# Mixture-of-experts stage: experts taken by token count, the last four on 64 token slots, weights split two pieces ahead

## The chip, the core and the metric

The kernel runs on one core of one Trainium2 chip. The metric is the device time of one execution in microseconds (us), the median of three runs. The core's engines work side by side, each with its own queue of instructions: TensorE (PE; its weight loads are listed as PEld), VectorE (DVE), ScalarE (ACT), GpSimd (POOL) and SyncE (SP), which here only issues transfers. Sixteen DMA engines carry what the queues issue.

## The reference

256 tokens of width 1024 go through a transformer block of two layers and then a second block of one layer. The part that the change touches most is the mixture of experts that ends the first block:

```
logits = (t @ w_router).astype(F32)                  # 8 experts
top_val, top_idx = lax.top_k(logits, TOP_K)          # 2 of them per token
top_w = jax.nn.softmax(top_val, axis=-1)
combine = jnp.sum(jax.nn.one_hot(top_idx, N_EXPERTS, dtype=F32) * top_w[..., None], axis=1)
for e in range(N_EXPERTS):
    gt, up = jnp.split(t @ w_gate_up[e], 2, axis=-1) # 1024 -> 2 x 3584
    y = (jax.nn.silu(gt) * up) @ w_down[e]           # 3584 -> 1024
    out = out + combine[:, e:e + 1].astype(t.dtype) * y
```

Each token needs two experts only, so an expert has some 64 tokens on the mean of the 256. The second block has an attention with a bias by relative position; its bias table of 8 x 384 numbers, copied to 128 rows of a scratch array in DRAM, is the other thing touched.

## The kernel before, in words

All weights are float32. TensorE multiplies in fp32r, and to keep the accuracy each factor is split into a high part H (a rounded copy, made on ACT) and a low part L (the rest, made on DVE; `parts`, lines 186 to 189). A product is three matmuls into one accumulator, H*H, H*L and L*H (`mm3`, lines 191 to 195): the 128 x 128 block of activations is the stationary factor, the 512 columns of weights move. `unit` (line 170) loads one piece of weights, 128 x 2048 numbers or 1 MB, into a buffer `raw`, and splits it in two halves of 1024 columns into `wH` (3 buffers) and `wL` (2 buffers). In the expert stage `raw` has 12 buffers in turns (`more_raw`, line 135): 5 of the ring, 5 of a pool of the stage, and 2 that are the second set of `hH` and `hL`.

In the expert stage the router's result is turned into `place`, the slot of each token among an expert's tokens. `pair` (line 988) gathers the tokens of two experts by matmuls with one-hot matrices `oh`, 128 slots each. For each of the 8 experts in the order of their numbers, and each of 7 slices j of 512 hidden columns, `up` (line 1070) makes gate and up product (4 pieces of `moe_w_gate_up`, 48 matmuls), then SiLU on ACT and the product on DVE (`act`), 4 transposes into `tp`, and the split into `aH` and `aL`; `down` (line 1105) of the slice before adds its 2 pieces of `moe_w_down` into two accumulators `acc` (24 matmuls). After an expert's last slice `scatter` (line 1130) splits the accumulators into `yH` and `yL`, multiplies with the transposed one-hot matrix and adds to the residual `xs` on DVE. The first gate product is made over all 256 tokens while the router's result is still on its way (`first_gates`, line 1049). An expert with more than 128 tokens would need a second pass, which stands behind a branch (`tc.If`, line 878) and would go over all eight experts again.

What stands behind what in an engine's queue is settled when the program is built; `issue_after(x)` keeps an instruction from being placed before x. In the dense layer ahead, `conditioning` (line 808) is work on the side: `side(j)` takes three steps of a generator per slice, and one of these steps is the copy of the bias table to 128 rows (line 859).

Of the kernel before, what the change touches and what calls it, by code (L numbers as in the profile page):

```python
# [10 lines left out]
F32 = mybir.dt.float32  # L11
# [19 lines left out]
RAW = 5  # L31
LEVELS = (64, 32, 16, 8, 4, 2, 1)
# [53 lines left out]
class Net:  # L86
# [47 lines left out]
    @contextmanager  # L134
    def more_raw(self, bufs, more):

        was, spare = self.ring, self.hp[1 - self.turn]
        with self.tc.tile_pool(name="more", bufs=more) as pool:
            more_ = lambda n: pool.tile([128, n], F32, name="raw", tag="raw")
            spare_ = [lambda n, tag=tag: spare.tile([128, n], F32, name="raw", tag=tag) for tag in ("hH", "hL")]  # L140
            turns = itertools.cycle([more_] * more + [was[0]] * bufs + spare_)
            self.ring = (lambda n: next(turns)(n)), *was[1:]
            yield
        self.ring = was
# [41 lines left out]
    def parts(self, H, L, src):  # L186

        self.high = self.nc.scalar.activation(H, src, AF.Copy)  # L188
        self.low = self.nc.vector.tensor_tensor(L, src, H.bitcast(F32), op=OP.subtract)  # L189
# [618 lines left out]
    def conditioning(self, sb, psum):  # L808
# [41 lines left out]
        def steps():  # L850
# [21 lines left out]
    def moe(self, f):  # L872
        nc, tc, A = self.nc, self.tc, self.A
        with self.stage("M", gu=2, acc=2) as (sb, psum):
            route = self.route(f, sb, psum)
            with self.more_raw(RAW, 5):
                self.experts(sb, psum, route, self.cst["iota"], f.x)
            with self.weights(1, 1, 1, 1024), tc.If(route["most"] > 128):

                iota2 = sb.tile([128, 128], F32, name="iota2", tag="before")  # L880
                nc.vector.tensor_scalar(iota2, self.cst["iota"], 128.0, None, op0=OP.add)
                self.experts(sb, psum, route, iota2)
# [13 lines left out]
    def route(self, f, sb, psum):  # L896
# [4 lines left out]
        before = sb.tile([128, NE, NE], F32, name="before", tag="before")  # L901
# [4 lines left out]
        nc.gpsimd.tensor_copy(ones, self.cst["ones"])  # L906
        hp = [sb.tile([128, 2, D], F32R, name=n) for n in ("hpH", "hpL")]
# [44 lines left out]
        route = dict(place=place, hp=hp, r=rp, r_token=r)  # L952

        def weights():
# [24 lines left out]
            most = sb.tile([128, 1], F32, name="most")  # L979
            nc.vector.tensor_reduce(most, ps[:, :NE], axis=AX.X, op=OP.max)  # L980
            most_i = sb.tile([128, 1], I32, name="most_i")
            nc.vector.tensor_copy(most_i, most)
            route["most"] = nc.values_load(most_i[0:1, 0:1], min_val=0, max_val=T)
# [4 lines left out]
    def pair(self, sb, psum, route, e, iota):  # L988
# [4 lines left out]
        oh = sb.tile([128, 2, 2, 128], F32R, name="oh")  # L993
        shape = [128, 2, 2, 128]
        nc.vector.tensor_tensor(oh, iota[:, None, None, :].to_broadcast(shape),
                                route["place"][:, :, e:e + 2, None].to_broadcast(shape), op=OP.is_equal)
        H, L = self.h_parts(other=False)
        g, hp = self.cols["moe_norm"], route["hp"]
        for c0 in range(0, KC, 2):
            ps = psum.tile([128, 512], F32, name="tp", tag="tp")  # L1000
            for k in (c0, c0 + 1):
                o = ps[:, (k - c0) * T:(k - c0 + 1) * T]
                for i in range(4):
                    nc.tensor.matmul(o, hp[i // 2][:, i % 2, k * 128:(k + 1) * 128],
                                     oh[:, i % 2].rearrange("p e s -> p (e s)"), start=i == 0, stop=i == 3)
                nc.scalar.activation(H[:, k], o, AF.Copy, scale=g[:, k:k + 1])  # L1006
                nc.vector.scalar_tensor_tensor(L[:, k], o, g[:, k:k + 1], H[:, k].bitcast(F32),
                                               op0=OP.mult, op1=OP.subtract)

        def later():  # L1010
            rs = sb.tile([128, 2], F32, name="r_slot", bufs=2)
            ps = psum.tile([128, 512], F32, name="r_ps", tag="tp")
            for i in range(4):
                nc.tensor.matmul(ps[:, i // 2 * 2:i // 2 * 2 + 2], oh[:, i % 2, i // 2], route["r"][:, i % 2],
                                 start=i % 2 == 0, stop=i % 2 == 1)
            nc.vector.tensor_reduce(rs, ps[:, :4].rearrange("p (e i) -> p e i", i=2), axis=AX.X, op=OP.add)
            return rs

        return (H, L), oh, later

    def experts(self, sb, psum, route, iota, x=None):
# [3 lines left out]
        W1, W2 = A["moe_w_gate_up"][0], A["moe_w_down"][0]  # L1025
        size = self.ring[2]
        ng = FE // 512
        acc, by = {}, {}

        def ohT(e):  # L1030

            if e % 2 == 0:
                by["ohT"] = sb.tile([128, 2, T], F32R, name="ohT")
                ps = psum.tile([128, 512], F32, name="tp", tag="tp")
                for i in range(4):
                    self.transpose(ps[:, i * 128:(i + 1) * 128], by["oh"][:, i % 2, i // 2].bitcast(F32))
                nc.scalar.copy(by["ohT"].rearrange("p e t -> p (e t)"), ps)
            return by["ohT"][:, e % 2]

        def halves(e, j, i):  # L1040

            n = size // 512
            c0 = i * FE + j * 512
            for k0 in range(0, KC, n):
                wH, wL = self.unit([(None, W1[e, k0 * 128:(k0 + n) * 128, c0:c0 + 512].rearrange(
                    "(c p) n -> p c n", p=128))], n, 512)
# [509 lines left out]
```

## Time and profile before

| | us |
|---|---|
| median of 3 runs (lowest to highest) | 1869.73 (1869.43 to 1871.19) |
| profiled execution | 1871.38 |
| its span, first to last instruction | 1869.2 |
| of it outside the span | 2.2 |
| expert stage, first gate matmul to the last addition to the residual | 514.5 to 1526.3 |

The page gives each engine's busy time, then the span in 40 slices. PE is busy for 97% of the span, DVE for 79%, ACT for 66%. Of the span, 1011.8 us lie in the expert stage. A matmul's duration in the trace overlaps that of the next one, so its price is the distance from one start to the next.

### The profile page before, as it was taken

To read this page: it belongs to the slowest core of one execution; us is meant where nothing else is said; L and a number is where in the kernel's file an instruction comes from. 1 tells how busy PE (TensorE), PEld (TensorE's weight loads), DVE (VectorE), ACT (ScalarE), POOL (GpSimd) and SP (SyncE) were. 2 spreads that over 40 slices of the span, in tenths; PEclk is the share of its full clock that TensorE was granted. 3 is DMA by queue.
4 is the path that set the end of the run, shared out by engine and by line. 5 is a ranking of instruction groups with operands and counts; after the bars stand their busy time and mean duration, and the time that the engine had idled before them with its cause. 6 is when DMAs were issued, how large, how long until landed. Compare 5 with 4: busy or idle time off the path is not lost. (4 is left out here: it accounts for less than half of the span.)

```text
span 1869.2 us, 23364 instructions
## 1 busy us (share of the span) xinstructions
PE 1809.2 (97%) x8491; PEld 1457.6 (78%) x8491; DVE 1477.4 (79%) x1819; ACT 1227.6 (66%) x1761; POOL 70.0 (4%) x107
## 2 busy tenths in 40 slices
PE   8999999999999999999999999999999979989997
PEld 6767787788778888788787887887887857778886
DVE  4857788676789999898988989888898876575555
ACT  5655444575678777777777777777787766555443
POOL 2002000110100000000000000000000010000001
PEclk9999999999999999999999999999999989999999
DMA  8537999642679999899999999998999945355551
GB/s 266 166 105 243 331 323 340 198 147 92 227 278 370 369 351 377 307 368 367 340 369 341 347 359 338 371 371 304 363 369 342 330 134 172 114 164 185 181 180 46
DMA packets 224938, 511.37 MB, mean 274 GB/s; under 512 B 10181, under 2 KB 35909, under 8 KB 221616
## 3 DMA queue, kind: packets, MB, share of 16 engines
q1 hardware_dynamic: 221872, 501.84, 75.8%
q0 software_dynamic: 2496, 7.10, 1.5%
q8 instruction: 69, 1.13, 0.2%
q10 hardware_dynamic: 448, 0.86, 0.1%
q14 instruction: 53, 0.43, 0.1%
HBM read 508.68 MB, written 2.66 MB: 274 GB/s over the span
## 5 line engine op out<-in xcount | busy, mean ns | idle before, releaser
L189 DVE TENSOR_TENSOR wL<-raw,wH 128x1024 fp32r<-128x1024 f32 (+1 forms) x1001 | 1072.2, 1117 | 199.8 <-issue 120.5
L188 ACT ACTIVATE wH<-raw 128x1024 fp32r<-128x1024 f32 (+1 forms) x1001 | 912.1, 969 | 252.5 <-PE gu L195 71.4
L193 PE MATMUL gu<-wH,hH 128*128 128x512 f32 x1192 | 468.0, 393 | 2.3 <-ACT hH L1006 2.3
L194 PE MATMUL gu<-wL,hH 128*128 128x512 f32 x1192 | 466.2, 391 | 3.1 <-DVE wL L189 3.0
L195 PE MATMUL gu<-wH,hL 128*128 128x512 f32 x1192 | 466.0, 391 | 0.0
L194 PEld LDWEIGHTS gu<-wL,hH 128*128 128x128 f32 x1192 | 224.5, 188 | 55.7 <-DVE wL L189 5.7
L195 PE MATMUL acc<-wH,aL 128*128 128x512 f32 x664 | 265.9, 401 | 0.0
L194 PE MATMUL acc<-wL,aH 128*128 128x512 f32 x664 | 264.0, 398 | 0.0
L193 PEld LDWEIGHTS gu<-wH,hH 128*128 128x128 f32 x1192 | 224.6, 188 | 50.3 <-ACT hH L1006 3.7
L195 PEld LDWEIGHTS gu<-wH,hL 128*128 128x128 f32 x1192 | 224.4, 188 | 46.1
L193 PE MATMUL acc<-wH,aH 128*128 128x512 f32 x664 | 257.3, 402 | 0.0
L193 PE MATMUL mm<-wH,hH 128*128 128x512 f32 (+1 forms) x384 | 152.5, 398 | 0.8 <-ACT hH L1484 0.5
L194 PE MATMUL mm<-wL,hH 128*128 128x512 f32 (+1 forms) x384 | 150.9, 393 | 0.0
L194 PEld LDWEIGHTS acc<-wL,aH 128*128 128x128 f32 x664 | 125.1, 188 | 32.3 <-DVE wL L189 4.1
L195 PE MATMUL mm<-wH,hL 128*128 128x512 f32 (+1 forms) x384 | 149.6, 391 | 0.0
L193 PEld LDWEIGHTS acc<-wH,aH 128*128 128x128 f32 x664 | 125.1, 188 | 26.2 <-issue 0.3
L195 PEld LDWEIGHTS acc<-wH,aL 128*128 128x128 f32 x664 | 125.1, 188 | 26.2 <-issue 0.2
L188 ACT ACTIVATE aH<-tp 128x512 fp32r<-128x512 f32 (+1 forms) x94 | 51.3, 545 | 121.4 <-PE tp L198 121.2
L193 PEld LDWEIGHTS mm<-wH,hH 128*128 128x128 f32 x384 | 73.7, 192 | 15.3 <-issue 1.7
L194 PEld LDWEIGHTS mm<-wL,hH 128*128 128x128 f32 x384 | 73.6, 192 | 14.6 <-issue 2.7
L195 PEld LDWEIGHTS mm<-wH,hL 128*128 128x128 f32 x384 | 73.4, 191 | 13.7 <-issue 1.7
L1093 DVE SCALAR_TENSOR_TENSOR act<-gu,r_slot,act 128x512 f32<-128x512 f32 x56 | 42.0, 750 | 49.1 <-PE gu L195 49.1
(437 smaller groups left out, 1415.8 us busy)
## 6 DMA issues: line engine op xcount, KB each, us to landing
raw<-in_moe_w_gate_up_dram SPq DMA_DIRECT2D x224, 1024.0 KB, 7.3
raw<-in_moe_w_down_dram SPq DMA_DIRECT2D x112, 1024.0 KB, 6.0
raw<-in_w_ff_dram SPq DMA_DIRECT2D x32, 1024.0 KB, 5.1
raw<-in_w_ada_dram SPq DMA_DIRECT2D x24, 1024.0 KB, 6.8
raw<-in_dense_w_gate_up_dram SPq DMA_DIRECT2D x44, 512.0 KB, 5.2
raw<-in_b_w_in_dram SPq DMA_DIRECT2D x12, 1024.0 KB, 5.1
raw<-in_w_in_dram SPq DMA_DIRECT2D x12, 1024.0 KB, 5.2
raw<-in_dense_w_down_dram SPq DMA_DIRECT2D x11, 1024.0 KB, 7.3
```

The lines of the kernel that those rows point to most:

```text
L188: self.high = self.nc.scalar.activation(H, src, AF.Copy)
L189: self.low = self.nc.vector.tensor_tensor(L, src, H.bitcast(F32), op=OP.subtract)
L193: mm(ps, xH, wH, start=start, stop=False)
L194: mm(ps, xH, wL, start=False, stop=False)
L195: mm(ps, xL, wH, start=False, stop=stop)
L1093: nc.vector.scalar_tensor_tensor(a, ps[1], r, a, op0=OP.mult, op1=OP.mult)
```

## The change

Six things are changed together.

- **Order of the experts.** Expert 0 stays first (its first gate product starts before the router's result is there); the other seven follow by falling number of tokens. DVE works the order out from the counts in 24 small operations behind the first slice (`order`), and SP loads the seven numbers and the largest count into registers; the address of every later piece of expert weights comes from such a register.
- **64 slots.** The last four experts in turn (`BIG_TURNS = 4`) have 64 slots. The stationary block then holds H in its first 64 columns and L in the other 64, so that one matmul with `wH` gives H*H in rows 0 to 63 and L*H in rows 64 to 127, and a second one with `wL` on 64 columns adds H*L: two matmuls for three. The two halves have to be added: for the gate by a copy to SBUF and a float32 matmul with a matrix `fold`, for the product behind the transposes (`both`), for the result by the scatter. The largest count is compared after 64 is added to those of the last four, so the second pass would run if one of the last four had more than 64 tokens.
- **Steps.** An expert's seven slices are taken in steps of 1, 2, 2 and 2; in a step of two a piece of `moe_w_gate_up` is 2 x 1024 columns, not 4 x 512.
- **Split ahead.** A piece is split whole (2048 columns), and two pieces ahead of the one that TensorE takes (`stream`, `ahead` = 2). `raw` has 10 buffers in turns, `wL` has 3. The evacuations of the accumulators (`act`, `aH`, `aL`, `yH`, `yL`, `xs`) stand behind these splits (`behind`, `put_off`).
- **Gathers.** Tokens are gathered for expert 0, for the next two, for the next one, and for the last four, not in four pairs.
- **Bias rows.** The copy of the bias table is made in 8 parts of 16 rows, one with each of the first 8 steps of the side work.

```
+BIG_TURNS = 4
...
+            spare_ = lambda n: spare.tile([128, n], F32, name="raw", tag="hL")
+            turns = itertools.cycle([more_] * more + [raw] * bufs + [spare_])
+            low_ = lambda n: whl[1].tile([128, n], F32R, name="wL")
+            spare_l = lambda n: spare.tile([128, n], F32R, name="wL", tag="hH")
+            lows = itertools.cycle([low_] * low + [spare_l])
...
+    def stream(self, sources, ahead):
+        nc = self.nc
+        raw_, (pH, lows), size = self.ring
+        low_ = lows if callable(lows) else lambda n: lows.tile([128, n], F32R, name="wL")
+        made = []
+        for src in sources:
+            raw = raw_(size)
+            view = lambda x: x.rearrange("p (c b) -> p c b", b=src.shape[-1])
+            nc.sync.dma_start(view(raw), src)
+            H = pH.tile([128, size], F32R, name="wH")
+            L = low_(size)
+            self.parts(H, L, raw)
+            made.append((view(H), view(L)))
+            if len(made) > ahead:
+                yield made.pop(0)
+        yield from made
...
-            nc.gpsimd.dma_start(self.skew, table[0].partition_broadcast(128))
-            yield
-            for seg in range(3):
-                yield from ada(seg)
-
+            copies = iter(range(0, 128, 16))
+            for _ in itertools.chain.from_iterable(ada(seg) for seg in range(3)):
+                i = next(copies, None)
+                if i is not None:
+                    nc.gpsimd.dma_start(self.skew[i:i + 16], table[0].partition_broadcast(16))
...
-            with self.more_raw(RAW, 5):
-                self.experts(sb, psum, route, self.cst["iota"], f.x)
+            with self.more_weights(RAW, 4, 2):
+                self.experts(sb, psum, route, self.cst["iota"], self.cst["iota"], 2, f.x)
             with self.weights(1, 1, 1, 1024), tc.If(route["most"] > 128):
...
+            nc.vector.tensor_scalar(cnt[:, 0:1], cnt[:, 0:1], 1000.0, None, op0=OP.add)
...
+            nc.vector.tensor_scalar(full[:, BIG_TURNS:], full[:, BIG_TURNS:], 64.0, None, op0=OP.add)
+            nc.vector.tensor_reduce(which[:, 0:1], full, axis=AX.X, op=OP.max)
+            whole = small("int", [NE], I32)
+            nc.vector.tensor_copy(whole, which)
+            sp = [mybir.EngineType.SP]
+            route["expert"] = [0] + [nc.values_load(whole[0:1, i:i + 1], engines=sp, min_val=0, max_val=NE - 1)
+                                     for i in range(1, NE)]
+            route["most"] = nc.values_load(whole[0:1, 0:1], min_val=0, max_val=T + 64)
...
+                if small:
+                    for x, d in ((H, slice(0, 2)), (L, slice(2, 4))):
+                        v = x[:, k].rearrange("p (e h s) -> p e h s", e=2, h=2)
+                        nc.scalar.activation(v[:, :, 0], o[:, d], AF.Copy, scale=g[:, k:k + 1])
+                        nc.vector.scalar_tensor_tensor(v[:, :, 1], o[:, d], g[:, k:k + 1], v[:, :, 0].bitcast(F32),
+                                                       op0=OP.mult, op1=OP.subtract)
...
+        steps = ((0,), (1, 2), (3, 4), (5, 6))
+        groups = ((0,), (1, 2), (3,), (4, 5, 6, 7))
...
+            pend = None
+            for e in range(NE):
+                for js in steps:
+                    yield from w1(e, js, 0)
+                    yield from w1(e, js, 1)
+                    if pend is not None:
+                        yield from w2(*pend)
+                    pend = e, js
+            yield from w2(*pend)
...
+        def behind():
+            with self.tc.issue_after(self.high.ins), self.tc.issue_after(self.low.ins):
+                yield
...
+        def product(ps, x, H, L, start, stop):
+
+            if len(x) == 2:
+                self.mm3(ps, *x, H, L, start, stop)
+                return
+            high = lambda: mm(ps, x[0], H, start=start, stop=stop)
+            if start:
+                high()
+            mm(ps[:64], x[0][:, :64], L, start=False, stop=False)
+            if not start:
+                high()
...
+            def fold():
+                for p in ps[0]:
+                    y = sb.tile([128, 512], F32, name="halves", tag="act", bufs=2)
+                    with behind():
+                        nc.scalar.copy(y, p)
+                    put_off(0, lambda p=p, y=y: mm(p, route["fold"], y, start=True, stop=True))
...
+                    if small:
+                        both = sb.tile([128, 4, 64], F32, name="both", tag="aL", bufs=2)
+                        nc.scalar.copy(both, pt[:, :, 64:])
+                        def add():
+                            with behind():
+                                nc.vector.tensor_tensor(both, pt[:, :, :64], both, op=OP.add)
+                            put_off(0, lambda: split(y[0][:, :, :64], y[0][:, :, 64:], both))
+                        put_off(0, add)
+                    else:
+                        self.split(*y, pt)
...
+                        if not started:
+                            activations()
+                            for g in range(len(js)):
+                                put_off(ahead - 1 + g, lambda g=g, parts=parts: parts(g))
+                            started = True
...
+                with behind():
+                    self.split(*y, acc[h])
+                put_off(ahead, lambda: scatter(h, y))
```

How the queues change, as the two programs are built. First VectorE, three slices in the middle of the expert numbered 5 before (`wL` is the low part of weights, `act` the product of the two halves, `aL` its low part):

```order
L189 TENSOR_TENSOR wL<-raw,wH 128x1024 x9
L1093 SCALAR_TENSOR_TENSOR act<-gu_9871,r_slot,act 128x512
L189 TENSOR_TENSOR wL<-raw,wH 128x1024 x2
L189 TENSOR_TENSOR aL<-tp,aH 128x512
L189 TENSOR_TENSOR wL<-raw,wH 128x1024 x10
```

And VectorE now, a step of two slices in the first of the last four turns (`both` adds the two halves, `aH<-both` is the low part):

```order
L215 TENSOR_TENSOR wL<-raw,wH 128x2048 x8
L1279 SCALAR_TENSOR_TENSOR act<-gu_8995,r_slot,act 128x512
L1279 SCALAR_TENSOR_TENSOR act<-gu_8996,r_slot,act 128x512
L215 TENSOR_TENSOR wL<-raw,wH 128x2048 x2
L1295 TENSOR_TENSOR both<-tp,both 128x256
L215 TENSOR_TENSOR wL<-raw,wH 128x2048
L1295 TENSOR_TENSOR both<-tp,both 128x256
L215 TENSOR_TENSOR aH<-both,aH 128x4x64
```

Between a product and what is made of it there stand now at least two whole pieces, and the work on a slice is three operations where there were two.

TensorE at the end of a gate product before, in expert 5:

```order
L193 MATMUL gu_10139<-wH,hH 128x512
L194 MATMUL gu_10139<-wL,hH 128x512
L195 MATMUL gu_10139<-wH,hL 128x512
L193 MATMUL acc_9828<-wH,aH 128x512
L193 MATMUL acc_9829<-wH,aH 128x512
L194 MATMUL acc_9828<-wL,aH 128x512
L195 MATMUL acc_9828<-wH,aL 128x512
```

And now, at the seam from gate (gu_8993, gu_8994) to up product (gu_8995, gu_8996) of the first of the last four turns:

```order
L1207 MATMUL gu_8995<-wH,hH 128x512
L1207 MATMUL gu_8996<-wH,hH 128x512
L1210 MATMUL gu_8995<-wL,hH 64x512 x2
L1207 MATMUL gu_8995<-wH,hH 128x512
L1210 MATMUL gu_8996<-wL,hH 64x512 x2
L1207 MATMUL gu_8996<-wH,hH 128x512
L1251 MATMUL gu_8993<-halves,fold 128x512
L1251 MATMUL gu_8994<-halves,fold 128x512
L1210 MATMUL gu_8995<-wL,hH 64x512
```

The third matmul of a product is gone, and the two matmuls that add the gate's halves stand a whole piece of the up product behind the gate.

## Rows read from the trace of the kernel before

**Rows 1.** The page, busy time of each engine over the whole span

```profile
PE 1809.2 (97%) x8491; PEld 1457.6 (78%) x8491; DVE 1477.4 (79%) x1819; ACT 1227.6 (66%) x1761; POOL 70.0 (4%) x107
```

**Rows 2.** Stretches: length, busy PE, PEld, DVE, ACT, POOL (count), PEclk, DMA share, GB/s

```profile
185.00:195.00 10.00, 10.00 (x47) 8.09 (x46) 9.90 (x10) 3.05 (x6) 0.55 (x1) 1.00 0.95 343
...
235.00:245.00 10.00, 10.00 (x45) 8.27 (x45) 9.25 (x8) 4.29 (x5) 1.01 (x2) 1.00 0.94 339
...
500.00:510.00 10.00, 10.00 (x50) 8.21 (x49) 7.57 (x10) 7.22 (x13) 0.00 (x0) 1.00 1.05 397
...
701.00:748.00 47.00, 47.00 (x212) 38.48 (x212) 42.85 (x40) 37.27 (x40) 0.00 (x0) 1.00 1.02 377
...
1042.00:1526.00 484.00, 478.41 (x2140) 386.36 (x2138) 429.06 (x415) 357.90 (x403) 0.00 (x0) 1.00 0.94 339
```

**Rows 3.** Who waited for whom, SP's DMA queue, 561 to 1496: total, times, longest

```profile
SPq L178 <- DVE wL L189: 773.7, 307, 8.2
```

**Rows 4.** Timeline of PE in the expert stage: start, us, engine, line, operation

```profile
514.50 0.40 PE L193 MATMUL gate<-wH,hH 128*128 128x512 f32 x1
...
1036.74 0.39 PE L195 MATMUL acc<-wH,aL 128*128 128x512 f32 x1
...
1044.16 0.39 PE L195 MATMUL gu<-wH,hL 128*128 128x512 f32 x1
...
1049.60 0.39 PE L195 MATMUL gu<-wH,hL 128*128 128x512 f32 x1
...
1051.23 0.60 PE L198 MATMUL tp<-cst,act 128*128 128x128 f32 x4
...
1052.14 0.39 PE L195 MATMUL acc<-wH,aL 128*128 128x512 f32 x1
...
1054.24 0.39 PE L195 MATMUL acc<-wH,aL 128*128 128x512 f32 x1
```

**Rows 5.** Timeline of DVE, expert 4 and the stage's end

```profile
1042.91 6.89 DVE L189 TENSOR_TENSOR wL<-raw,wH 128x1024 fp32r<-128x1024 f32 x6
...
1524.93 1.41 DVE L1142 SCALAR_TENSOR_TENSOR xs<-tp,comb,xs 128x512 f32<-128x512 f32 x2 [0.59 <-PE tp L1141]
```

**Rows 6.** Groups by line and shape, DVE and ACT: count, busy us, mean ns

```profile
L1093 DVE SCALAR_TENSOR_TENSOR act<-gu,r_slot,act 128x512 f32<-128x512 f32 x56 | 42.0, 750 | 49.1 <-PE gu L195 49.1
...
L189 DVE TENSOR_TENSOR aL<-tp,aH 128x512 fp32r<-128x512 f32 x72 | 49.3, 684 | 0.3 <-ACT aH L188 0.3
...
L1142 DVE SCALAR_TENSOR_TENSOR xs<-tp,comb,xs 128x512 f32<-128x512 f32 x32 | 22.6, 746 | 3.4 <-PE tp L1141 3.1
...
L189 DVE TENSOR_TENSOR aL<-tp,aH 128x256 fp32r<-128x256 f32 x22 | 9.1, 418 | 1.1 <-ACT aH L188 1.0
...
L189 DVE TENSOR_TENSOR ada_L<-ada_acc,ada_H 128x2048 fp32r<-128x2048 f32 x3 | 6.9, 2286 | 0.6 <-ACT ada_H L188 0.6
...
L188 ACT ACTIVATE ada_H<-ada_acc 128x2048 fp32r<-128x2048 f32 x3 | 5.7, 1915 | 7.6 <-DVE ada_acc L834 7.6
```

**Rows 7.** Groups by line and shape, PE: contraction*columns of the stationary, moving, mean ns

```profile
L193 PE MATMUL router<-hH,wrH 128*8 128x256 f32 x8 | 2.3, 290 | 0.0
...
L1004 PE MATMUL tp<-oh,hpL 128*128 128x256 f32 x64 | 13.1, 286 | 0.0
...
L310 PE MATMUL mem_s<-kvT,mem_qT 64*128 64x256 f32 x32 | 10.0, 428 | 0.0
```

**Rows 8.** The bias copy on POOL, PE's wait and the stretch around that wait

```profile
185.47 0.55 POOL L859 DMA_DIRECT2D skew<-skew_row  x1 [6.44 <-DMA skew_row<-skew_st]
...
208.61 0.69 PE L198 MATMUL tp<-cst,act 128*128 128x128 f32 x2 [4.20 <-DVE act L549]
...
205.00:215.00 10.00, 6.39 (x25) 5.19 (x25) 8.36 (x8) 4.83 (x6) 0.00 (x0) 0.83 0.97 343
```

**Rows 9.** Line 983: what SP spends on one register load and one address

```profile
L983 SPq TENSOR_LOAD <-most_i x1: 466/466/466, 546.5 to 546.5; - x1
...
L983 SPq FUSED_REGOPS  x1: 182/182/182, 547.0 to 547.0; - x1
```

More of the change, by code (lines that the diff above doesn't have):

```diff
@@ new lines, in experts, with take, put_off @@
+        stream = self.stream(sources(), ahead)
+        def take():
+            for i in range(len(later)):
+                later[i][0] -= 1
+            due = [x for x in later if x[0] < 0]
+            later[:] = [x for x in later if x[0] >= 0]
+            for x in due:
+                x[1]()
+            return next(stream)
+        def put_off(n, f):
+            later.append([n, f])
+        @contextmanager
+        def behind():
+            with self.tc.issue_after(self.high.ins), self.tc.issue_after(self.low.ins):
+                yield
@@ L1038, in ohT @@
[L1038 to L1046, printed above, removed]
-                yield from ((k0 + k, wH[:, k], wL[:, k]) for k in range(n))
+                for i in range(2 * n):
+                    self.transpose(ps[:, i * 128:(i + 1) * 128], oh[:, i % 2, i0 + i // 2].bitcast(F32))
@@ L1121, in experts @@
[L1121 to L1141 removed]
+                        product(acc[h], [y[:, k] for y in a], H[:, k - k0, d], L[:, k - k0, d],
+                                j == 0 and k == 0, j == steps[-1][-1] and k == 3)
@@ new lines, in down, with finish, half, scatter @@
+                yield
+        def finish(e):
+            acc, o = by.pop("acc"), ohT(e)
+            def half(h):
+                y = [sb.tile([128, 512], F32R, name=n) for n in ("yH", "yL")]
+                with behind():
+                    self.split(*y, acc[h])
+                put_off(ahead, lambda: scatter(h, y))
+            def scatter(h, y):
+                self.scatter(psum, h, y, o, route["comb"][:, :, e:e + 1], behind)
+                if h == 0:
+                    half(1)
+            half(0)
@@ new lines, in experts @@
+        made = {}
+        pend = None
+        for e, js in itertools.product(range(NE), steps):
+            activations, parts = up(e, js)
+            if js == steps[-1] and e + 1 in first:
+                ohT(e)
+                fetch(first[e + 1])
+            if pend is None:
+                activations()
+                for g in range(len(js)):
+                    parts(g)
+                if "comb" not in route:
+                    with self.tc.issue_after(self.low.ins):
+                        route["weights"]()
+            else:
+                started = False
+                for j in pend[1]:
+                    for _ in down(pend[0], j):
+                        if not started:
+                            activations()
+                            for g in range(len(js)):
+                                put_off(ahead - 1 + g, lambda g=g, parts=parts: parts(g))
+                            started = True
+                if pend[1] == steps[-1]:
+                    finish(pend[0])
+            pend = e, js
@@ new lines, in experts, with scatter @@
+        while later:
+            later.pop(0)[1]()
+        for j in pend[1]:
+            for _ in down(pend[0], j):
+                pass
+        finish(pend[0])
+        while later:
+            later.pop(0)[1]()
+    def scatter(self, psum, h, y, ohT, w, behind):
+        nc = self.nc
+        d = slice(h * 512, (h + 1) * 512)
+        for t in range(2):
+            ps = psum.tile([128, 512], F32, name="tp", tag="tp")
+            s = ohT[:, t * 128:(t + 1) * 128]
+            nc.tensor.matmul(ps, s, y[0], start=True, stop=False)
+            nc.tensor.matmul(ps, s, y[1], start=False, stop=True)
+            with behind():
```

277 lines of the change are left out of this document (168 added, 109 removed).

## The prediction

> **What bounds the kernel now.** I read the page's busy times first, then the stretches, then who waited for whom, then the timeline of TensorE and VectorE, and last the groups by line and shape, for durations. TensorE (PE) is busy for 97% of the span [rows 1]. The expert stage runs from PE's first gate matmul at 514.5 to the last addition to the residual, 1524.93 + 1.41 = 1526.3: 1011.8 us [rows 4, 5]. In its second half PE is busy for 478.4 of 484 us, but VectorE (DVE) is close behind with 429.1 [rows 2], so whatever PE gives up can be used only until DVE is full. The loads lead: SP spent 773.7 us of 935 waiting for DVE to free a buffer [rows 3].
>
> A slice can be counted from the timeline. From 1044.16 to 1049.60 stand 24 matmuls of the up product, 0.2267 each; from 1052.14 to 1054.24 nine of the down product, 0.2333 each; four transposes add some 0.45 [rows 4]. A slice of 48 + 24 matmuls is 10.88 + 5.60 + 0.45 = 16.93 us, an expert 118.5. Eight are 948 us of the 1011.8.
>
> **The change, part by part.** *TensorE, last four experts.* Two matmuls instead of three make 224 x 0.2267 + 112 x 0.2333 = 76.9 us per expert. That the one with 64 stationary columns costs as much as the one with 128 I take from the router's matmuls: 8 stationary columns 290 ns, 128 columns 286 ns, both moving 256 [rows 7]. The fold is a plain float32 matmul of 512 columns, which the trace does not show; the nearest row moves 256 in 428 ns where the split kind takes 286 [rows 7]. Its price lies between 0.23 (as any other) and 0.86 (twice the whole 428); I take 0.52, since 286 ns stands for a distance of 0.12 and 428 so for 0.26 per 256 columns. Seven folds are 3.6, seven slices of transposes 3.2, the scatter's 8 matmuls 2.1: 85.8 us per expert, 32.7 less than now. Its cover is DVE, below, so this alone is not the gain.
>
> *VectorE, last four experts.* Six back-to-back halves take 6.89 us and a lone one 1.22, so one starts every 1.134 and durations overlap by 0.08 [rows 5]. The whole piece exists in the trace as the split of `ada_acc`: 2.286 long [rows 6], 2.206 from start to start, against 2 x 1.134 = 2.268. An expert's 42 pieces are 92.7 us. Evacuations, each less 0.08 [rows 6]: `act` 0.67, and for `both` and the low part of `aH` 0.335 each by the row of 256 columns (418 ns): 1.34 per slice where there were 1.27. Scatter: four additions of 0.67 and two splits of 0.60, 3.9. That makes 92.7 + 9.4 + 3.9 = 106.0 us per expert: DVE loses almost nothing and becomes the bound, 106.0 against PE's 85.8. ScalarE has at most 42 x 1.915 = 80 us of splits [rows 6] and some 12 of copies; it stays behind DVE.
>
> *The last four in place.* In the built program DVE has split 175 of the 336 pieces when PE takes the fourth expert's last one. What is left: 161 x 2.206 = 355.2, 28 slices x 1.34 = 37.5, four scatters 15.5, together 408.2 us; then a tail of about 7 (the last piece's matmuls, and a scatter in two halves, one after the other, as now). In stretches in which DVE was the waited-for engine it was busy for 9.25 to 9.90 of 10 us [rows 2]; I take 0.96: 425 + 7 = 432. Before, the same way runs from 1036.74 + 0.39 = 1037.1 to 1526.3: 489.2 us [rows 4, 5]. Gain 57. With DVE never waiting it would be 415 (gain 74); the lower end is the loads' (below).
>
> *The loads, last four.* 161 pieces less the 9 that wait loaded are 152, or 159.4 MB. At the rate of one slice now, 6.29 MB in 16.93 us = 371 GB/s, they take 429 us; at the best long stretch, 377, 423; at the best short one, 397, 401 [rows 2]. The 371 was set by PE, not by the queue [rows 3], so I take the loads as just hidden by the 425, and 12 us for landing and tail where they are not: 441.
>
> The Trainium skill, "DMA: Bandwidth & Descriptors", "Specifications", gives 358 GB/s as the limit of HBM per core; by it the loads take 445 us, the last four 457, and the total would be 1827. The stretch of 377 over 47 us speaks against that limit here. The same page ("iDMA fabric") has a lone stream of 1 MiB loads with 4 KiB rows, the shape that most pieces now get, at 408.7; by that they take 390 and are hidden.
>
> *First four experts.* The same 504 matmuls each; PE stays the bound. Until the fourth's last product there are now 1037.1 - 514.5 = 522.6 us: 4 x 118.5, the first gates' 24 further matmuls and 4 selecting ones 6.3, three gathers of 32 x 0.12 = 3.8, three scatters of 2.1, 48 matmuls of the next expert 10.9: 509 of work, 13.7 of waits. Afterwards: 4 x 118.5, 6.3, two gathers of 3.8 and two of one expert each (32 x 0.11 by the transposes' distance) 3.5, three scatters 6.3, 32 matmuls of the next expert 7.3: 508.5. The waits can stay (0) or go (13.7), since scatter and gather now stand behind splits that are ready; I take half: gain 7.
>
> *Order and registers.* 24 small DVE operations fall into expert 0, where DVE has 118.5 - 106 = 12 us to spare: cost 0, some 4 us if that cover were gone. SP's eight register loads (0.47 + 0.18 and checks, some 0.7 each [rows 9], 5.5 together) hold up SP's queue; behind them stand 15 more pieces of expert 0. SP stops there before the 28th piece and DVE gives the result behind the 19th; a buffer for the 28th is free behind the 18th. A delay of one piece and 5.5 us meets up to nine loaded pieces, 25 us: hidden. Each later address costs SP 0.18, per piece of 2.5 us or more: hidden.
>
> *Bias rows.* The copy goes out at 185.47; at 208.61 PE has waited 4.20 us for DVE, which waited for weights, and in 205 to 215 it starts 25 matmuls, not the 46 or so of its neighbours, part of the time at the lower clock (mean 0.83) [rows 2, 8]. 21 x 0.2267 = 4.8. In eight parts the copy can cost nothing or the same, spread: gain 0 to 4.8, I take 4.
>
> **Sum.** 57 + 7 + 4 = 68 us. The span goes from 1869.2 to 1801, the profiled execution from 1871.4 to 1803; the median of the runs lies 1.7 below that execution: 1802.
>
> **Rivals.** *Loads take over.* Ten buffers for twelve, and a rate never seen for long. For it: the DMA engines are busy all the time at 377 already (share 1.02); against: 397 in a short stretch [rows 2]. 441 for the last four gives 1811; at the mean of the second half, 339, they would need 470 + 12 and give 1852.
>
> *Evacuations take over.* In the last four a slice has a longer chain (copy, fold, SiLU, product, transposes, copy, add, split), and DVE takes its queue in order: a product that is late holds back the splits behind it. For it: `act` waited 49.1 us for PE in 56 turns [rows 6]. Against: that was while PE was the bound, and two pieces now stand in between, over 4 us. 16 steps with two stops of 1.5 us are 48: 480, total 1850.
>
> *TensorE falls to its lower clock (slower than before).* PE will wait some (106 - 86) / 42 = 0.5 us at every piece. After the wait of 4.2 us the granted clock of 205 to 215 was 0.83 [rows 8], so some of that time was at 1.2 GHz. If the last four ran there throughout, PE would need 4 x 2 x 85.8 = 686 us: total 2055. It decides once PE needs more than 489 + 11 = 500 for the four, 1.46 times its 85.8. Against: waits of half a microsecond are an eighth of the one that did it, and at half speed PE would be busy all the time.
>
> *The second pass runs.* Counted from the reference on its own inputs, the experts have 55, 74, 53, 86, 71, 54, 55 and 64 tokens: turns 0, 3, 1, 4 and then 64, 55, 54, 53. The largest of the last four fills its slots exactly, 64 + 64 = 128 is not above 128. One token more and everything runs again, 352 MB or some 950 us at 371 GB/s: about 2750.
>
> **Chances.** My forecast 0.68, loads 0.15, evacuations 0.11, clock 0.04, second pass 0.02. My forecast's own range is 1777 (gains of 74, 14 and 5) to 1817 (the last four at 441, no wait gone in the first four). With the loads at their milder end and a part of the evacuations the range that holds 8 in 10 is 1783 to 1831. A measurement here tells 0.2% (3.7 us) from no change. Faster needs only that DVE, the loads or the chain leave 4 of 68 us: 0.93; same 0.02; slower 0.05.
>
> **What would show it.** DVE at 95% or more in the last four experts and PE near 80%, at a granted clock near 1; some 432 us from the fourth expert's last product to the end; DMA near 390 GB/s there; the whole-piece split at 2.28 us; PE's wait near 208 gone. Wrong would be: DVE idle there waiting for `raw` (loads), or for `gu` and `tp` (chain), a clock well under 1, or PE's 64-column matmuls at a distance other than 0.227.

## The result, and the profile after

The changed kernel takes **1816.77 us** (median of 4 runs, 1815.36 to 1818.86), before in the same measurement 1869.58: a ratio of 0.9718, with a 95% interval from 0.9701 to 0.9735. Forecast were 1802, with a range from 1783 to 1831. The profiled execution took 1817.69 us, its span fell from 1869.2 to 1815.9, that is by 53.3 us where the sum gave 68.

Stage by stage, from the first gate matmul, the last `acc` matmul of the fourth turn and the last addition to the residual in the two traces (us):

| stretch | before | after | gain | forecast gain |
|---|---|---|---|---|
| up to the first gate matmul | 514.5 | 511.0 | 3.5 | 4 |
| first four experts | 522.6 | 527.5 | -4.9 | 7 |
| last four experts | 489.2 | 435.2 | 54.0 | 57 |
| behind them | 342.9 | 342.2 | 0.7 | 0 |

The windows of the changed kernel that answer to [rows 2] and [rows 8]: columns are the window and its length, then busy us of each engine with its instructions, the granted clock, the DMA engines' share and rate.

```profile
205.00:215.00 10.00, 9.47 (x43) 7.75 (x44) 8.43 (x10) 4.57 (x6) 0.00 (x0) 1.00 1.03 369
510.00:525.00 15.00, 15.00 (x81) 11.70 (x81) 12.05 (x25) 8.64 (x14) 0.73 (x1) 1.00 0.68 218
525.00:540.00 15.00, 12.00 (x50) 9.85 (x50) 6.08 (x11) 6.18 (x12) 0.00 (x0) 0.77 0.38 133
540.00:1035.00 495.00, 492.81 (x2256) 401.89 (x2255) 442.25 (x322) 366.69 (x271) 0.00 (x0) 1.00 0.95 352
1100.00:1300.00 200.00, 174.56 (x708) 108.16 (x707) 194.42 (x127) 165.59 (x133) 0.00 (x0) 1.00 1.03 403
1450.00:1475.00 25.00, 17.05 (x56) 9.90 (x54) 16.40 (x16) 14.38 (x19) 0.00 (x0) 0.84 0.38 129
```

In the last four (1100 to 1300) VectorE (DVE) is busy for 97% of the time, TensorE (PE) for 87%, at a granted clock of 1.00; an expert takes 109.4 us there. Who waits in that window (us in all, times, longest):

```profile
PEld gu L1210 <- DVE wL L215: 34.7, 39, 1.4
PE gu L1210 <- DVE wL L215: 18.6, 29, 0.9
```

PE now waits for the low parts of the weights, as forecast: the bound has gone to DVE. The loads run at 403 GB/s with a share of 1.03 in the same window, so they could be a second bound. Against that, SyncE (SP), which issues them, waits for DVE to free a buffer, for more than half of the 200 us:

```profile
SPq L161 <- DVE wL L215: 115.4, 59, 3.5
```

Apart from the stage's tail, one window has both idle time of PE and a low clock, 525 to 540. It lies in the first four experts, for which a gain was forecast. The experiments go after these two.

### The profile page after: what moved, and what is told of

It is laid out like the page before. It is cut to its first block, busy times and chain, and to the rows that moved or that the text cites. A ratio compares the mean times of both kernels' runs of the same rounds, so it can differ in the third digit from the quotient of the medians.

```text
span 1815.9 us, 21998 instructions
## 1 busy us (share of the span) xinstructions
PE 1706.0 (94%) x7875; PEld 1304.0 (72%) x7875; DVE 1453.5 (80%) x1545; ACT 1208.2 (67%) x1490; POOL 79.3 (4%) x116
## 3 DMA queue, kind: packets, MB, share of 16 engines
q8 instruction: 64, 1.05, 0.2%
## 5 line engine op out<-in xcount | busy, mean ns | idle before, releaser
L215 DVE TENSOR_TENSOR wL<-raw,wH 128x2048 fp32r<-128x2048 f32 (+2 forms) x665 | 1047.0, 1604 | 222.7 <-issue 87.9
L215 ACT ACTIVATE wH<-raw 128x2048 fp32r<-128x2048 f32 (+2 forms) x665 | 886.4, 1364 | 313.8 <-PE gu L221 120.1
L220 PE MATMUL gu<-wL,hH 128*128 128x512 f32 x744 | 292.6, 394 | 0.1
L221 PE MATMUL gu<-wH,hL 128*128 128x512 f32 x744 | 291.7, 393 | 0.0
L219 PE MATMUL gu<-wH,hH 128*128 128x512 f32 x744 | 286.5, 395 | 2.2 <-ACT hH L1093 2.2
L221 PE MATMUL acc<-wH,aL 128*128 128x512 f32 x440 | 174.7, 397 | 0.0
L220 PE MATMUL acc<-wL,aH 128*128 128x512 f32 x440 | 174.2, 396 | 0.3 <-DVE wL L215 0.3
L1210 PE MATMUL gu<-wL,hL 128*64 128x512 f32 x224 | 88.7, 413 | 20.0 <-DVE wL L215 19.5
L1210 PE MATMUL acc<-wL,aH 128*64 128x512 f32 x224 | 91.9, 417 | 16.0 <-DVE wL L215 11.9
L1210 PE MATMUL gu<-wL,hH 128*64 128x512 f32 x224 | 88.6, 413 | 17.4 <-DVE wL L215 16.9
L1207 PE MATMUL gu<-wH,hH 128*128 128x512 f32 x224 | 85.6, 396 | 0.5 <-ACT wH L215 0.5
```

The source lines that it names most:

```text
L215: return self.nc.scalar.activation(H, src, AF.Copy), self.nc.vector.tensor_tensor(L, src, H.bitcast(F32), op=OP.subtract)
L219: mm(ps, xH, wH, start=start, stop=False)
L220: mm(ps, xH, wL, start=False, stop=False)
L221: mm(ps, xL, wH, start=False, stop=stop)
L1207: high = lambda: mm(ps, x[0], H, start=start, stop=stop)
L1210: mm(ps[:64], x[0][:, :64], L, start=False, stop=False)
```

## Experiments

Theory: VectorE bounds the last four, the 64 slots carry the gain, and what the first four lost lies in the 15 us after 525. Rivals: the loads bound the last four; the gain comes from the splits ahead; the loss lies at the later gathers.

### The slots alone: all experts on 128

```
-BIG_TURNS = 4
+BIG_TURNS = 8
-groups = ((0,), (1, 2), (3,), (4, 5, 6, 7))
+groups = ((0,), (1, 2), (3,), (4, 5), (6, 7))
```

> All eight experts on 128 slots; the order by counts, the splits two pieces ahead and the bias rows in parts stay. Theory (the 64 slots carry the whole gain, the other parts together come out at about nothing): the bias rows give 3.5 us, the first four experts take 5 us more than before, the last four are again 489 us, so the time is that of before, 1867 to 1876 us. Rival (the splits ahead give some of the gain by themselves, since waits at the seams go): PE's own work for an expert is 118.5 us, so the last four could fall to 4 x 118.5 + 7 = 481 and the time to 1858 to 1864 us.

Measured: 1864.17 us, ratio to before 0.9969 [0.9958, 0.9980]. This lies just above the rival's range and below the theory's. By stretches: first four 527.1, as in the changed kernel, last four 482.6. So, with the rest of the change in place, the 64 slots bring 47.4 of the 54.0 us, and the rest brings 6.6 without them: the forecast had put all 57 down to the slots.

### The splits two ahead

```
-self.experts(sb, psum, route, self.cst["iota"], self.cst["iota"], 2, f.x)
+self.experts(sb, psum, route, self.cst["iota"], self.cst["iota"], 0, f.x)
```

> Weights split not two pieces ahead but each when it is taken; 64 slots stay. Theory (two ready pieces between a product and its evacuation are what keeps the longer chain of the last four out of sight): 16 steps stop twice for about 1.5 us, 48 us, so 1850 to 1870 us and VectorE well under 95% busy in the last four. Rival (the scheduler moves ready splits ahead by itself and the three weight buffers allow no more than two ahead anyway): 1815 to 1825 us.

Measured: 1856.83 us, 0.9933 [0.9913, 0.9953]. The last four take 468.4 instead of 435.2, the first four 531.5 instead of 527.5. Busy times in the same window as above:

```profile
1100.00:1300.00 200.00, 162.89 (x644) 98.14 (x643) 177.33 (x114) 152.75 (x121) 0.00 (x0) 0.99 0.99 367
```

DVE falls to 89%, PE to 81%. The theory holds: without ready pieces in between, the longer chain of copy, fold and product shows, at 33 us where the forecast's rival "evacuations take over" had 48. The 64 slots need the splits ahead to be worth what they are: without them the last four gain 20.8 us against the kernel before, the change without the slots 6.6, and both together 54.0, so the two do not simply add up.

### The bias rows in one copy

```
-copies = iter(range(0, 128, 16))  ...  self.skew[i:i + 16]
+nc.gpsimd.dma_start(self.skew, table[0].partition_broadcast(128))
```

> The bias rows again in one copy of 128 rows, all else as changed. Theory (the copy holds up the weight loads for one piece): PE waits some 4 us near 208 us of the span again, and the time is 3 to 4 us more than the changed kernel's, 1820 to 1821 us. Rival (the dense part's 3.5 us came from something else that moved, such as the fold's constants on POOL): 1816 to 1818 us.

Measured: 1818.96 us, 0.9726 [0.9712, 0.9740]; by the ratios 1.5 us more than the changed kernel, which the intervals don't separate. The traces do more: the first gate matmul stands at 514.5, as before, against 511.0. The wait of [rows 8] is back, and so is its window:

```profile
206.71 0.44 PE L224 MATMUL tp<-cst,act 128*128 128x128 f32 x2 [4.20 <-DVE act L575]
```
```profile
205.00:215.00 10.00, 8.29 (x31) 6.66 (x32) 8.19 (x9) 5.47 (x7) 0.00 (x0) 0.83 0.86 292
```

The copy in parts is not free: in the changed kernel the wait at that place is shorter, not gone,

```profile
205.53 0.44 PE L224 MATMUL tp<-cst,act 128*128 128x128 f32 x2 [1.37 <-DVE act L575]
```

and in the twelve profiled executions with the copy in parts it is 0.9 to 2.6 us. In one of these, with 2.5 us, the first gate matmul starts at 514.2; the other eleven have it at 509.1 to 511.8. The mean of the twelve, 510.6, against 514.5 in both executions with one copy, puts the copy's price at 3.9 us up to there; of this the time of the whole kernel shows 1.5 to 2.2.

### An edge at the first gather

The start of the stage in the changed kernel, ScalarE (ACT) and then TensorE: start, duration, instruction, and in brackets what was waited for.

```profile
524.75 0.67 ACT L1227 ACTIVATE act<-gate,rstd 128x512 f32<-128x512 f32 x1
525.32 1.90 ACT L215 ACTIVATE wH<-raw 128x2048 fp32r<-128x2048 f32 x1
527.12 0.61 ACT L1093 ACTIVATE hH<-tp,c_moe_norm 128x128 fp32r<-128x128 f32 x2
```
```profile
527.52 0.50 PE L219 MATMUL gu<-wH,hH 128*128 128x512 f32 x1 [2.21 <-ACT hH L1093]
527.86 0.40 PE L220 MATMUL gu<-wL,hH 128*128 128x512 f32 x1
528.09 0.47 PE L1273 MATMUL gu<-aH,oh 128*128 128x512 f32 x1
528.36 0.63 PE L1273 MATMUL gu<-aL,oh 128*128 128x512 f32 x1
528.79 0.63 PE L1273 MATMUL gu<-aH,oh 128*128 128x512 f32 x1
529.22 1.05 PE L219 MATMUL gu<-wH,hH 128*128 128x512 f32 x2
```

A weight split of 1.90 us stands ahead of the gather's first evacuation in ACT's queue. PE has nothing else and waits 2.2 us (2.48 from one start to the next); 0.8 us after it starts again its matmuls stand 0.43 apart instead of 0.23, the lower clock of 1.2 GHz.

```
 high = nc.scalar.activation(H[:, k, :cols], ...)
+if k == 3: self.hold = high
 ...
+with self.tc.issue_after(hold.ins):   # the next weight piece
     return next(stream)
```

> One scheduling edge added: the third weight piece behind the first gates' own two is split only behind the fourth evacuation of the first gather. Theory (the first four experts lost their time at the stage's start, where PE waited 2.48 us for an evacuation that stood behind a 1.90 us weight split on ScalarE, and then ran some 7 us at 1.2 GHz): the wait goes, the clock stays at 1.00, and the time falls by 5 to 7 us against the changed kernel, to 1810 to 1812 us. Rival (the loss lies at the later gathers and in the additional gather of a single expert): no change, 1815 to 1818 us.

Measured: 1814.00 us, 0.9699 [0.9686, 0.9713], an interval that still overlaps the changed kernel's; the first four take 524.9 instead of 527.5, a gain of 2.6 in place, under the 5 to 7 expected. Other runs bear the place out: from the first gate matmul to the first expert's last `acc` matmul, the five profiled executions that have this edge (this run and four that follow) take 151.7 to 152.9 us, the seven that split two ahead without it 154.2 to 155.9. The window shows why it is not more:

```profile
525.00:540.00 15.00, 13.15 (x63) 10.83 (x63) 8.89 (x18) 9.41 (x14) 0.00 (x0) 0.89 0.36 133
```

PE waits 1.05 us for the evacuation, now behind the gates' own, and the clock still falls for a while. So the place is right, and the edge mends half of it. A second one puts the gates' evacuations behind the gather's too (`with issue_after(hold): gates = gates()`):

> Besides the third weight piece, the first gates' own evacuations stand behind the fourth evacuation of the first gather, and TensorE gathers the whole of the first expert at once. Theory (what is left of the start's loss after the first such edge is 1 us of waiting behind the gates' evacuations and 3 us at 1.2 GHz): the time is 2 to 4 us under that of the kernel with the one edge, 1809 to 1812 us. Rival (the gather waits for its own evacuations, two banks deep, wherever it stands): 1813 to 1816 us.

Measured: 1813.49 us, 0.9709 [0.9684, 0.9733], first four 525.5: no more than the first edge. The rival holds: the gather waits for its own evacuations, now twice for 0.40 us. That is little, and yet the clock falls as far as in the changed kernel:

```profile
525.00:540.00 15.00, 14.17 (x60) 11.94 (x61) 8.38 (x12) 11.52 (x15) 0.00 (x0) 0.77 0.23 78
```

So the length of the wait does not by itself tell how much of the low clock follows, and how to keep the clock up there stays open.

### The order as constants

```
-expert = lambda e: 0 if e == 0 else route["expert"][e]
+expert = lambda e: (0, 3, 1, 4, 7, 6, 5, 2)[e]
```

> The order of the experts is written into the addresses of the loads as constants (the order that the counts give); the order is still worked out on VectorE for the places and weights, but no register of SP is read for an address. Theory (SP's registers are hidden behind the loads that lead): within 2 us of the changed kernel, 1815 to 1819 us. Rival (the delay of SP in the first expert is part of what the first four experts lost): 3 to 5 us less, 1811 to 1814 us.

Measured: 1815.70 us, 0.9716 [0.9693, 0.9739]; first four 528.1, last four 435.2. The registers cost nothing that can be measured.

### VectorE or the loads: half of the one, half of the other, half of both

```
 if small:   # VectorE: low part of the first 1024 columns, read twice
-    self.parts(H, L, raw)
+    ... nc.vector.tensor_tensor(half(L), half(raw), half(H), op=OP.subtract)
```
```
 if small:   # loads: the first half of the piece, split twice
-    nc.sync.dma_start(view(raw), src)
+    nc.sync.dma_start(view(raw)[:, :c], src[:, :c])
```

> In the last four experts VectorE makes the low part of only half of each weight piece (1024 columns, about 1.2 us instead of 2.29), and TensorE reads that half twice; loads, ScalarE and TensorE's instructions stay. Theory (VectorE is the bound there, 97 of 100 us busy): its work falls from 106 to some 60 us per expert, the next bound is the loads (159.4 MB at the 403 GB/s of the last four, 395 us) or ScalarE (4 x 92 us) with seams and tail: the last four fall from 435 to 385 to 410 us and the time to 1767 to 1792 us. Rival (the loads are the bound, the DMA engines' share is 1.02 in the same stretch): no change, 1812 to 1818 us.

> In the last four experts each load brings only half of a piece (0.5 MB), and both splits read that half twice; the splits' sizes and TensorE's instructions stay. Theory (VectorE is the bound): no change beyond 3 us, 1812 to 1818 us. Rival (the loads are the bound or slow the engines down): the last four fall towards TensorE's and VectorE's own work, 415 us, and the time by 15 us or more, to 1800 or less.

> In the last four experts both at once: half of each piece is loaded, and VectorE makes the low part of that half only; ScalarE and TensorE as in the changed kernel. Theory (in the last four two bounds lie within 2%: VectorE with 106.9 us an expert, as the run with half the loads showed, and the loads with 108 to 109, as the run with half of VectorE's splits showed; ScalarE is the next with 95 to 96, as in the first expert of that run): 4 x 95.5 us and the same ends, so the last four take 378 to 386 us and the time is 1760 to 1770 us. Rival (there is a third limit near 108 us, such as the chain of copy, fold and product): at least 1785 us.

Measured: 1797.71 us (0.9622 [0.9590, 0.9654]), 1806.82 us (0.9662 [0.9635, 0.9689]) and 1742.29 us (0.9318 [0.9302, 0.9333]). Neither theory got the first two right: the time fell by 19 us with half of the splits, 10 with half of the loads, and by 74 with both, where 47 to 57 were expected. The same window of the three, in that order:

```profile
1100.00:1300.00 200.00, 183.55 (x750) 114.34 (x749) 122.85 (x131) 174.08 (x139) 0.00 (x0) 1.00 1.03 407
```
```profile
1100.00:1300.00 200.00, 181.59 (x726) 109.63 (x723) 198.06 (x128) 170.07 (x135) 0.00 (x0) 1.00 0.69 206
```
```profile
1100.00:1300.00 200.00, 198.63 (x857) 133.23 (x856) 141.59 (x153) 196.42 (x162) 0.00 (x0) 1.00 0.79 244
```

With half of the splits DVE is busy for 61%, yet from one expert to the next it still takes 107.6 and 108.8 us; only the first of the four, which has the loaded pieces to draw on, takes 95.1. The loads run at 407 GB/s, and an expert's 44.04 MB at 407 are 108.2 us. ACT waits for them:

```profile
ACT wH L175 <- DMA raw<-in_moe_w_gate_up_dram: 8.2, 18, 0.7
ACT wH L175 <- DMA raw<-in_moe_w_down_dram: 7.9, 13, 0.7
```

With half of the loads DVE is at 99% and an expert takes 106.9. This does not show that the loads bound the changed kernel. There no engine waits for a load in this window, and each piece had landed 11 to 15 us before ACT began to split it (issues, landings and splits of the trace, one by one); with half of the splits 46 of 70 pieces were split within 0.3 us of landing. And the edit did more than halve the loads: in the program that was built with it, ACT's queue has another order, with one more weight split ahead of the copy to `both`. For that copy ACT waits in the changed kernel,

```profile
ACT both L1291 <- PE tp L224: 11.6, 7, 1.9
```

with half of the loads not at all, and DVE's waiting for ACT's high parts falls from 5.6 to 1.9 us of the 200. So the 10 us may come from the order; no run halves the loads and keeps it. With both halved an expert takes 90.6 to 92.2, PE and ACT at 98 to 99%; the 95.5 expected came from the one expert above that follows the seam from 128 to 64 slots.

In the last four, then, DVE is the bound: 106.4 of the 109.4 us an expert are its work (97.2%), and the rest is waiting for ACT's high parts. The loads are the limit that comes next, 1% away: with half of DVE's splits they bind at 108.2. Two limits do lie within 2% of each other, as the last expectation has it, but only DVE's is reached.

The prediction had weighed the Trainium skill's limit of 358 GB/s ("DMA: Bandwidth & Descriptors", "Specifications"). Here 403 and 407 GB/s stand over 200 us, so the measurement decides against that limit; the 408.7 that the same page has for a lone stream ("iDMA fabric") agrees with the ceiling seen.

### Three versions meant to be better

GpSimd (POOL) takes a part of the low parts in the last four: 256 of 2048 columns of each piece, or the whole of every eighth.

```
+self.low = nc.vector.tensor_tensor(L[:, :1792], ...)
+nc.gpsimd.tensor_tensor(L[:, 1792:], raw[:, 1792:], H[:, 1792:], op=OP.subtract)
```

> A candidate for a better kernel. With the edge at the first gather; in the last four experts GpSimd makes the low part of the last 256 of each piece's 2048 columns, VectorE the other 1792. Theory (VectorE relieved by 42 x 0.27 = 11 us an expert, the loads then bind at 108 us after the lead of loaded pieces is used up in the first of the four): 12 to 18 us from the last four and 3 us at the start, 1796 to 1802 us. Rival (GpSimd and VectorE hinder each other at SBUF, or TensorE waits for GpSimd's part): 1815 us or more, with VectorE's 1792 columns longer than 2.0 us.

> The other candidate: as that one, but GpSimd makes the whole low part of every eighth piece of the last four. Theory: the same relief of 11 to 12 us an expert, less some waits of TensorE for GpSimd's longer operation (about 1.34 us for 512 columns, so some 4 to 5 us for 2048): 1798 to 1806 us. Rival (each of GpSimd's operations stops TensorE and the three buffers behind it for 3 us or more, or slows VectorE): 1813 us or more.

Measured: 1837.50 us (0.9830 [0.9814, 0.9847]) and 1857.08 us (0.9925 [0.9908, 0.9941]), both slower than the changed kernel; the rivals hold. In the second, PE waits up to 3.0 us for POOL's pieces, and DVE's whole split takes 2.44 us. Groups of the first by shape, 1100 to 1300 (busy us, mean ns):

```profile
L168 DVE TENSOR_TENSOR wL<-raw,wH 128x1792 fp32r<-128x1792 f32 x74 | 172.3, 2366 | 5.8 <-ACT wH L167 5.8
L222 DVE TENSOR_TENSOR aH<-both,aH 128x256 fp32r<-128x256 f32 x12 | 8.7, 724 | 0.0
```

DVE's 1792 columns take 2.37 us beside POOL, longer than 2048 alone (2.29), and the split of 256 columns 0.72 instead of 0.42. The work taken from DVE came back as slower work on DVE: 42 x 0.08 + 7 x 0.30 = 5.5 us an expert more, and an expert takes 115.0 instead of 109.4. The Trainium skill has a rule that bears on it: by "SBUF — State Buffer", "SBUF: two separate sides", VectorE's operations with two inputs in SBUF and GpSimd's that read SBUF exclude each other, and the loser waits for the whole instruction. The durations agree in kind; they don't show a full block, which the 1.59 us of each of POOL's operations would be: 1792 columns alone would take an estimated 2.00 us (2.29 x 1792 / 2048), so 0.37 us of it shows on each of DVE's splits.

The last version leaves POOL alone, keeps the edge at the gather, and takes work off DVE by PE, which has time to spare: the fold matrix adds the halves while it transposes.

```
-self.transpose(pt[:, c * 128:(c + 1) * 128], a[:, c * 128:(c + 1) * 128])
+mm(pt[:, c * 64:(c + 1) * 64], a[:, c * 128:(c + 1) * 128], route["fold"][:, :64], start=True, stop=True)
 ...
-nc.scalar.copy(both, pt[:, :, 64:])  ...  nc.vector.tensor_tensor(both, pt[:, :, :64], both, op=OP.add)
+self.split(y[0][:, :, :64], y[0][:, :, 64:], pt)
```

> A third candidate. With the edge at the first gather; in the last four experts TensorE transposes a slice's product and adds its two halves in one step (four plain matmuls by the folding matrix of 64 columns in place of four transposes), so ScalarE's copy (0.37 us) and VectorE's addition (0.42 us) of every slice go, and the splits read PSUM. Theory (VectorE and the loads bind within 2% of each other): VectorE's work falls by 7 x 0.34 = 2.4 us an expert to 104.5, the loads then bind at 108 to 108.5 us once their lead is used up; some 4 us in the first of the four and 1 us in each other, with 3 us at the start: 1806 to 1810 us. Rival (the loads alone bind already, or the splits from PSUM hold VectorE up): the start's 3 us only, 1812 to 1816 us.

Measured: **1806.68 us**, 0.9672 [0.9657, 0.9686]: faster than both kernels, by 8.6 us (ratios 0.9718 and 0.9672) against the changed one, whose interval it doesn't touch. By the ratios 3.6 of the 8.6 us are the edge; the other 5.0 are the new step, whose interval touches that of the edge alone.

```profile
1100.00:1300.00 200.00, 180.00 (x766) 116.06 (x767) 192.20 (x115) 164.39 (x122) 0.00 (x0) 1.00 1.03 407
```

The last four fall to 425.9 us (434.2 with the edge alone), the tail with them: the last interval between experts is 90.9 us, 96.2 in the changed kernel. An expert takes 108.2 us. The number was expected, but not for its reason: the loads would take 108.2 too, yet no engine waits for one in this window, each piece had landed 8.5 us or more before its split, and SP waits 157 of the 200 us for buffers that DVE frees. DVE's work is 104.0 us an expert, near the 104.5 expected, and its idle time in the window, 7.8 us, is waiting for ACT's high parts.

## Why the prediction was right, and where it was off

The forecast lay 15 us too low, and the range held it; 12 of the 15 are the first four experts, 3 the last four.

**Last four: right, 54.0 for 57.** DVE became the bound at 97% (forecast 96%), the clock stayed at 1.00 although PE waited in pieces of up to 0.9 us, the whole-piece split takes 2.286 us, and 432 us forecast stand against 435.2. "I take the loads as just hidden" held, with little to spare: each piece lay ready 11 us or more before its split, but with less work on DVE the loads bind at 108.2 us an expert, 1% under the 109.4 measured.

**The fold was mis-sized and hidden.** The chosen 0.52 was the wrong place in the range; the upper end was right. The row it was worked out from [rows 7] has 32 records for 16 matmuls (DVE and ACT read 16 products there): a plain float32 matmul stands in the trace as two records, and 428 ns was one of them. The fold shows the same:

```profile
1077.18 1.88 PE L1251 MATMUL gu<-halves,fold 128*128 128x512 f32 x4
1078.49 0.80 PE L1210 MATMUL gu<-wL,hH 128*64 128x512 f32 x1
```

Two folds are four records, 0.428 apart (the trace of single instructions has 1077.18, 1077.61, 1078.04, 1078.47), 0.86 us a fold, so 6.0 us an expert instead of 3.6. PE had that to spare. (Four passes of the array for true float32, as the Trainium skill has it in "FP8 and Floating Point Precision", "TensorE Precision Notes", are an estimated 4 x 0.227 = 0.91 by the split kind's distance; the trace, with 0.86, is 6% under it.) The matmul with 64 stationary columns costs what one with 128 does, as taken from [rows 7]; the six that alternate in pairs from 1038.61 on stand 0.23 apart:

```profile
1038.61 0.62 PE L1210 MATMUL gu<-wL,hH 128*64 128x512 f32 x2
1039.06 0.62 PE L1207 MATMUL gu<-wH,hH 128*128 128x512 f32 x2
1039.53 0.61 PE L1210 MATMUL gu<-wL,hH 128*64 128x512 f32 x2
```

**First four: the step that failed, 12 us.** "The waits can stay (0) or go (13.7) ... I take half: gain 7." Most of the 13.7 were no waits. They were the remainder of a count of matmuls, and PE's own idle time in that stretch was 3.75 us, in nine places; counted from start to start these nine are 5.2 us, since a matmul's duration overlaps the next. Some 6 us more lie in 65 places where the next matmul starts about 0.1 us later than usual and no idle time is recorded. Before and after, first gate matmul to the fourth expert's end:

```profile
514.00:1038.00 524.00, 520.25 (x2377) 422.50 (x2376) 469.10 (x487) 398.16 (x451) 0.73 (x1) 1.00 0.97 349
```
```profile
511.00:1038.00 527.00, 521.81 (x2389) 424.92 (x2388) 461.83 (x358) 382.74 (x296) 0.73 (x1) 0.99 0.93 342
```

So no more than some 5 us could go. Instead idle time rose by 1.4 to 5.2, 3.0 of it at the start, and a clock of 0.77 over 15 us at the start is 6.9 us at half speed, 3.45 us of lost work: 1.4 + 3.45 = 4.9, the whole loss. The forecast priced the lower clock as a rival for the last four alone, and did not look at what the whole-piece split (1.90 us for 2048 columns) does to an evacuation behind it on ACT. The experiment with the edge shows the place and gives back half; that all of the loss would go was not shown, since neither edge kept the clock up.

**Bias rows, order and registers.** 3.5 for 4, though the wait near 208 is not gone, as the forecast had it, but 1.37 us for 4.20; and nothing for 0: with constants in place of registers the time stays.

**Rivals.** "Loads take over" did not come (1811 and 1852 forecast, at 371 and 339 GB/s; the rate was 403 and every piece lay ready), though it is the limit that stands next. That 1811 lies nearer to the 1816.77 measured than the forecast's 1802 is chance: the first four moved the time there. "Evacuations take over" did not come, and would have without the splits ahead. The clock fell, but at the start of the stage and for 7 us. The second pass did not run.

## What to carry to other kernels

Before a wait is put into a sum as something that can go, read the engine's idle time of that stretch: a remainder between counted work and elapsed time is for the most part not a wait, and can't be won back. DMA engines that are busy all the time, at a share of 1.03, do not show that the loads bind: look whether any engine waits for a load, and how long a piece lies ready before it is read. When the bound and the next limit are within a few per cent, halve each alone and both together; before such a run is read, see that the order of the queues stayed as it was. A larger piece of work on a queue is also a longer delay for whatever short evacuation stands behind it: look for the places where an engine has nothing else to do just then.

## What had not been expected of the hardware

- GpSimd's float32 subtraction of 256 columns beside VectorE's slowed that engine: 1792 columns 2.37 us, where 2048 alone take 2.29, and 256 columns 0.72 where 0.42.
- The loads held 407 GB/s over 200 us when DVE's work was halved, with 1 MiB pieces; 377 was the best long stretch before [rows 2].
- A plain float32 matmul of 512 columns shows as two records 0.428 us apart, 3.8 times the 0.227 us of one of the split kind.
- At the start of the stage PE ran at 1.2 GHz for 6.8 to 10.2 us after a wait of 2.0 to 2.2 us (seven executions without an edge), for 3.4 to 6.8 us after a wait of 1.1 us (four with the first edge alone), and for 6.8 us where it had waited only 0.40 us twice (both edges), while many waits of up to 0.9 us in the last four left the clock at 1.00. The length of the wait did not decide it; what did is open.
